# Cached rows of the depthwise convolution first, from their own buffer, and separate input buffers for the convolution of VectorE and of TensorE

## The chip, the cores and the metric

The kernel runs on one core of a Trainium2 chip. The core has a matrix engine (TensorE, PE in the rows), a vector engine (VectorE, DVE), a scalar engine (ScalarE, ACT), GpSimd (POOL) and SyncE (SP), which issues transfers; ScalarE and GpSimd issue transfers as well. Each engine works through its own instructions in order and waits for the others by semaphores. The metric is the time of one execution on the device, in microseconds; less is better.

## The reference

The program is one inference step of a decoder trunk with two layers, for a prompt of 512 tokens and 8 sequences of 4 new tokens each, 544 tokens of 1024 channels in all. The change lies in the first operation of layer 0, a convolution module:

```python
def conformer_conv(h, prev, w_pw1, b_pw1, w_dw, b_dw, ln_g, ln_b, w_pw2, b_pw2):
    u = h @ w_pw1 + b_pw1
    a, g = jnp.split(u, 2, axis=-1)
    u = a * jax.nn.sigmoid(g)
    if prev is None:
        prev = jnp.zeros((u.shape[0], CONV_W - 1, u.shape[2]), u.dtype)
    full = jnp.concatenate([prev.astype(u.dtype), u], axis=1)
    y = lax.conv_general_dilated(full, w_dw[:, None, :].astype(u.dtype), (1,), 'VALID',
                                 dimension_numbers=('NWC', 'WIO', 'NWC'),
                                 feature_group_count=u.shape[-1]) + b_dw
    y = jax.nn.silu(layernorm(y, ln_g, ln_b))
    return y @ w_pw2 + b_pw2, full[:, -(CONV_W - 1):]
```

The filter has CONV_W = 31 taps for each channel. The prompt starts from zeros; each of the 8 sequences starts from 30 cached rows, `state_conv` (8 x 30 x 1024 numbers, 960 KB). The rows that enter the module are normalised and modulated, `h = rmsnorm(x) * (1 + scale) + shift`, where scale, shift and the gate on the result are products of a conditioning vector with `w_ada`. A feed-forward block, projections of keys and values, a compression of cached rows by `w_phi1`, attention and a second feed-forward block follow.

## The kernel before

Channels lie on the 128 partitions, so the 1024 channels are 8 tiles. Matrix products are made in three passes of split numbers: `weights` loads 512 KB into `raw` (4 buffers), ScalarE makes the high part `whi` (L168), VectorE the low part `wlo` (L169), and `products` (L182, L184) multiplies high with high, high with low and low with high. The input is split in the same way: for each of 8 channel tiles VectorE makes `ht` (L542) and `h_lo` (L545), ScalarE `h_hi`. The small `ts` steps of GpSimd (L555, L557, L558) do the modulation for the 32 tokens of the sequences, which the products need for their second part of each row.

`gated_units` makes the convolution's input, one unit for each channel tile f = 0 to 7: 96 matmuls (two products, the gate and the value), the sigmoid on ScalarE, then `up` (L660) and `un` (L663) on VectorE. `up` is the tile for the 512 prompt tokens with 30 zeros ahead, `un` holds the new tokens of the sequences. Between units TensorE does pieces of the modulation, `ada_steps` (L449), whose loads use the `raw` buffers as well.

The convolution of the prompt is divided. For f = 0, 1, 2 VectorE does it, 31 operations for each tile (L736, L738), in `depthwise`. For f = 3 to 7 (`PE_CONV`) TensorE does it in `conv_products`: `up` goes out to DRAM (`up_d`) and comes back as a tile `xt` of shifted rows, GpSimd builds tap matrices `wd4` (L692), and 32 matmuls on quarters of the array (L700; 64 in the trace) make the sum.

The cached rows' share of the sequences' convolution is made in `state_parts`: a load of `state_conv`, 16 transposes on TensorE, four copies (L428), and for each channel tile and each half of the sequences a multiplication on GpSimd into `pr` (L435, two buffers) and a reduction on VectorE into `ys0` (L437), so 16 of each. It runs in the pool "setup". When this pool is closed the pool "compress" takes its place in the buffer: `w1` with the weights of the compression (16 loads of 128 KB, L974), eight small loads `hk` (L993) with the transpose `peT` of them on VectorE (L995), and the gathered cache rows `nat` (L1000) with their transposes (L1013). A tile of "compress" that lies where a tile of "setup" lay waits until that one is no longer read.

The order on each engine is set by a scheduler that plays the program through when the kernel is built; a piece may be put off by a lower priority, and a transfer can be told to be issued behind another one (`issue_after`). Transfers of SyncE and of GpSimd are issued in the order of their queues; one that has to wait holds up those behind it.

Of the kernel before, what the change touches and what calls it, by code (L numbers as in the profile page):

```python
# [7 lines left out]
F32 = mybir.dt.float32  # L8
# [6 lines left out]
P = 128  # L15
D = 1024
KT = D // P
SEQ = 512
# [10 lines left out]
CW = 31  # L29
# [12 lines left out]

TAIL_K = 2
NSTEP = 4
NF = 2
EARLY = 2
SEVEN = (8, 4)
NX = NB + 2
# [5 lines left out]
PE_CONV = (3, 4, 5, 6, 7)  # L54
# [58 lines left out]
class Kernel:  # L113
# [300 lines left out]

    def state_parts(self, sp):

        two = sp.tile([P, 4 * D + 64], F32, name="xt")
        sc = two[:120, :2 * D].rearrange("p (a d) -> p a d", a=2)
        with self.tc.issue_after(self.first_weights):
            self.sy.dma_start(sc, self.A["state_conv"].rearrange("l (a b) w d -> (l b w) a d", a=2))  # L420
        us = two[:, 2 * D:].rearrange("p (f b w) -> p f b w", f=KT, b=NB)
        self.g.memset(us[:, :, :, CW - 1:], 0.0)
        for a in range(2):
            for f0 in range(0, KT, 4):
                pt = self.bank()
                for f in range(4):
                    self.transpose(pt[:, f * 120:(f + 1) * 120], sc[:, a, (f0 + f) * P:(f0 + f + 1) * P])
                self.s.copy(us[:, f0:f0 + 4, a * 4:(a + 1) * 4, :CW - 1],  # L428
                            pt[:, :480].rearrange("p (f b w) -> p f b w", f=4, b=4))
        for f in range(KT):  # L430
            for b0 in range(0, NB, 4):
                uv = us[:, f, b0:b0 + 4]
                win = bass.AP(tensor=uv.tensor, offset=uv.offset, ap=[list(uv.ap[0]), [CW + DS - 2, 4], [1, DS], [1, CW - 1]])
                pr = sp.tile([P, 4, DS, CW - 1], F32, name="pr", bufs=2)
                self.g.tensor_tensor(out=pr, in0=win, in1=self.w_dw[:, :CW - 1, f].unsqueeze(1).unsqueeze(1)  # L435
                                     .broadcast_to([P, 4, DS, CW - 1]), op=ALU.mult)
                self.v.tensor_reduce(out=self.ys0[:, f, b0 * DS:(b0 + 4) * DS], in_=pr.rearrange("p b t w -> p (b t) w"),  # L437
                                     axis=AX.X, op=ALU.add)
# [190 lines left out]
    def gated_units(self, pool, between):  # L629
# [7 lines left out]
        self.ups = []  # L637
        convs = []
        for f in range(KT):
            if f == NF:  # L640
                self.first_weights = self.last_weights
            if f == STATE:
                yield
            cols = [wsrc[:, :, c * D + f * P:c * D + (f + 1) * P] for c in (1, 0)]
# [2 lines left out]
            else:  # L647
# [2 lines left out]
                    next(between, None)  # L650
                pg = self.product(wg, self.h_hi, self.h_lo, KT)
                pa = self.product(wa, self.h_hi, self.h_lo, KT)
            up = pool.tile([P, CW + SEQ], F32, name="up", bufs=4)
            self.ups.append(up)
            g.memset(up[:, :CW - 1], 0.0)
            g.memset(up[:, CW - 1 + SEQ:], 0.0)
# [20 lines left out]
    def conv_products(self, pool, f):  # L677


        n = SEQ + 28  # L680
        up, i = self.ups[f], PE_CONV.index(f)
        vs = self.compress_pool.tile([P, 4, n], F32, name="xt", bufs=3)
        ud = self.up_d[i]
        self.g.dma_start(ud, up)
        for t in range(4):
            src = bass.AP(tensor=ud.tensor, offset=ud.offset + t, ap=[[CW + SEQ, 32], [32 * (CW + SEQ), 4], [1, n]])
            self.g.dma_start(vs[32 * t:32 * t + 32], src)
        wds = []
        for q0 in range(0, 8, 4):

            wd = pool.tile([P, 4, 4, 32], F32, name="wd4", bufs=3)
            self.g.tensor_tensor(out=wd, in0=self.tap.unsqueeze(1).unsqueeze(1).broadcast_to([P, 4, 4, 32]),  # L692
                                 in1=self.w4[:, i, :, q0:q0 + 4].unsqueeze(3).broadcast_to([P, 4, 4, 32]), op=ALU.mult)
            wds.append(wd)

        yield
        pt = self.bank()
        for q in range(8):
            for gg in range(4):
                self.te.matmul(pt[32 * gg:32 * gg + 32, :], wds[q // 4][:, gg, q % 4], vs[:, gg, 4 * q:4 * q + SEQ], start=q == 0, stop=q == 7)  # L700
        self.s.activation(self.y[:, f, :SEQ], pt, AF.Identity, bias=self.b_dw[:, f:f + 1])
        yield
# [42 lines left out]
    def conv_states(self, pool):  # L745
# [2 lines left out]
        g.tensor_copy(uc.rearrange("p f (b t) -> p f b t", t=DS), self.un[:, :, :, DS - 1:])  # L748
        for f0 in range(0, KT, 4):

            both = pool.tile([P, 4, 4, 32], F32, name="wd4", bufs=3).rearrange("p a b n -> p (a b n)")
            cs, cn = both[:32], both[32:32 + NS]
            for f in range(4):
                pt = self.bank("b")
# [861 lines left out]
    def run(self):  # L1616
        tc, A = self.tc, self.A

        def sbuf(name, side="left"):
            return tc.tile_pool(name=name, bufs=1, side=side, reuse_waits="tile")  # L1620

        with sbuf("const") as self.cp, sbuf("norm") as self.np, \
# [17 lines left out]
            with sbuf("conv") as pool:  # L1640
                self.ys0 = pool.tile([P, KT, NS], F32, name="ys0")
                self.conv_pool = pool
                with sbuf("setup", "right") as sp:
                    self.setup(sp)
                    between = self.ada_steps(0, 2)
                    ada1 = itertools.chain(*(self.ada_steps(1, part) for part in (1, 0, 2)))
                    units_ = self.gated_units(pool, between)
                    next(units_)
                    self.state_parts(sp)
                compressing = sbuf("compress", "right")  # L1650
                self.compress_pool = compressing.__enter__()
                next(units_)
# [80 lines left out]
            with sbuf("ffn1") as pool:  # L1733
                u_hi, u_lo = [pool.tile([P, KT, TOK + NX], F32R, name=n, bufs=1) for n in ("a_hi", "a_lo")]
                self.unscaled_shift(3, u_hi, u_lo)
                for f in range(KT):
                    w = self.weights(wsrc[:, :, f * P:(f + 1) * P])
# [44 lines left out]
```

## Time and profile before

| | |
|---|---|
| runs, us | 1664.57, 1669.18, 1670.47; median 1669.18 |
| profiled execution, us | 1666.17, of which the span of the trace is 1664.4 |
| mean granted TensorE clock | 0.972 |
| TensorE busy | 1553.0 us (93%) in 12423 matmuls |
| VectorE busy | 1097.8 us (66%) |
| ScalarE busy | 695.2 us (42%) |
| GpSimd busy | 230.9 us (14%) |

The busy shares are averages over the whole program; the units and the convolution stand in its first 345 us. The chain of waits is followed back from the last instruction: at each step it shows what released the next one.

### The profile page before, as it was taken

What the parts mean: (1) busy time and instruction counts of PE and PEld (TensorE: products, weight loads), DVE (VectorE), ACT (ScalarE), POOL (GpSimd) and SP (SyncE); (2) the same over time, 40 slices, a digit from 0 to 9 for tenths busy, and PEclk for the clock granted to TensorE, in tenths of its full rate; (3) what the DMA queues carried; (4) which work ended last, traced back from release to release, by engine and by line L of the source; (5) the groups of instructions that cost most, each with busy time, mean ns of one, the idle gap of its engine ahead of it and who ended that gap; (6) DMA issues with size and microseconds to landing.
All of it is one profiled execution on the core that took longest, in us unless ns stands there. A gap on an engine that the chain in (4) does not pass through costs nothing.

```text
span 1664.4 us, 31574 instructions
## 1 busy us (share of the span) xinstructions
PE 1553.0 (93%) x12423; PEld 1359.1 (82%) x12423; DVE 1097.8 (66%) x2338; ACT 695.2 (42%) x1443; POOL 230.9 (14%) x267
## 2 busy tenths in 40 slices
PE   6889769999998889999999899999999999999997
PEld 3788337989987888999987777655689999999997
DVE  2799545473338888577657644867856964884866
ACT  4422016232122344245445322746745552552554
POOL 3045420021131021101111000000001210110010
PEclk8899978999999999999999999999999999999999
DMA  8655885374389999933869996747222472333231
GB/s 266 168 145 130 189 242 174 105 237 144 116 199 321 308 300 313 315 103 96 197 206 296 267 272 198 224 149 235 66 64 77 152 227 83 96 109 95 76 93 64
DMA packets 315327, 296.05 MB, mean 178 GB/s; under 512 B 15843, under 2 KB 275053, under 8 KB 310939
## 3 DMA queue, kind: packets, MB, share of 16 engines
q1 hardware_dynamic: 304507, 237.24, 48.7%
q0 software_dynamic: 10368, 56.56, 10.6%
q8 instruction: 98, 1.61, 0.4%
q14 instruction: 50, 0.41, 0.1%
q10 hardware_dynamic: 304, 0.23, 0.1%
HBM read 257.39 MB, written 45.76 MB: 182 GB/s over the span
## 4 chain that ended last, share of the span: by engine, by line
PE 70%; DMA 12%; DVE 11%; issue 3%; ACT 2%; SPq 1%; POOL 0%; ACTq 0%; DVEq 0%
PE g L184 19%; PE g L182 18%; PE g L246 9%; PE t L246 4%; PE t L154 3%; PE t L1019 3%; PE o L1500 2%; DMA raw<-in_w_ada_dram 2%; DVE wlo L195 2%; DMA raw<-in_w_up_dram 2%; PE a L449 2%; DVE y L738 1%; DMA w<-in_w_phi_dram 1%; PE t L1349 1%; PE sc L1479 1%
## 5 line engine op out<-in xcount | busy, mean ns | idle before, releaser
L168 ACT CAST whi<-raw 128x512 fp32r<-128x512 f32 x250 | 149.6, 606 | 399.5 <-PE g L184 269.7
L169 DVE TENSOR_TENSOR wlo<-raw,whi 128x512 fp32r<-128x512 f32 x250 | 175.9, 707 | 142.3 <-ACT whi L168 139.8
L182 PE MATMUL g<-h_hi,whi 128*128 128x256 f32 (+1 forms) x584 | 170.6, 293 | 13.3 <-DVE un L663 8.2
L184 PE MATMUL g<-h_hi,whi 128*128 128x288 f32 (+4 forms) x584 | 174.2, 299 | 0.7 <-ACT h_hi L559 0.7
L184 PE MATMUL g<-h_lo,whi 128*128 128x288 f32 (+4 forms) x584 | 174.0, 298 | 0.4 <-DVE h_lo L560 0.4
L184 PE MATMUL g<-h_hi,wlo 128*128 128x288 f32 (+4 forms) x584 | 173.9, 298 | 0.0
L182 PE MATMUL g<-h_lo,whi 128*128 128x256 f32 (+1 forms) x584 | 168.0, 288 | 0.0
L182 PE MATMUL g<-h_hi,wlo 128*128 128x256 f32 (+1 forms) x584 | 167.8, 287 | 0.0
L182 PEld LDWEIGHTS g<-h_hi,whi 128*128 128x128 f32 x584 | 111.7, 192 | 25.5 <-issue 15.2
L246 PE MATMUL g<-T,whi 128*128 128x272 f32 x656 | 127.7, 291 | 4.5 <-DVE sg L260 3.9
L194 ACT CAST whi<-s 128x512 fp32r<-128x512 f32 x128 | 79.4, 620 | 104.9 <-PE g L246 58.7
L182 PE MATMUL g<-a_hi,whi 128*128 128x256 f32 (+1 forms) x372 | 107.2, 289 | 11.9 <-ACT a_hi L889 5.1
L184 PEld LDWEIGHTS g<-h_hi,whi 128*128 128x128 f32 x584 | 111.8, 192 | 4.0 <-issue 2.9
L184 PEld LDWEIGHTS g<-h_hi,wlo 128*128 128x128 f32 x584 | 111.7, 191 | 3.4 <-issue 3.4
L182 PEld LDWEIGHTS g<-h_lo,whi 128*128 128x128 f32 x584 | 112.1, 192 | 2.8 <-issue 2.7
L184 PEld LDWEIGHTS g<-h_lo,whi 128*128 128x128 f32 x584 | 111.5, 191 | 2.9 <-issue 2.1
L182 PEld LDWEIGHTS g<-h_hi,wlo 128*128 128x128 f32 x584 | 111.9, 192 | 1.3 <-issue 1.0
L184 PE MATMUL g<-a_hi,wlo 128*128 128x288 f32 (+1 forms) x372 | 110.4, 297 | 0.0
L184 PE MATMUL g<-a_hi,whi 128*128 128x288 f32 (+1 forms) x372 | 110.4, 297 | 0.0
L184 PE MATMUL g<-a_lo,whi 128*128 128x288 f32 (+1 forms) x372 | 109.9, 296 | 0.0
L246 PEld LDWEIGHTS g<-T,whi 128*128 128x128 f32 x656 | 103.5, 189 | 6.9 <-DVE sg L260 3.3
L182 PE MATMUL g<-a_hi,wlo 128*128 128x256 f32 (+1 forms) x372 | 105.6, 284 | 2.4 <-DVE wlo L169 2.4
(495 smaller groups left out, 4113.8 us busy)
## 6 DMA issues: line engine op xcount, KB each, us to landing
raw<-in_w_ada_dram SPq DMA_DIRECT2D x96, 512.0 KB
raw<-in_w_gate_dram SPq DMA_DIRECT2D x44, 512.0 KB
raw<-in_w_up_dram SPq DMA_DIRECT2D x44, 512.0 KB
raw<-in_w_down_dram SPq DMA_DIRECT2D x32, 512.0 KB
raw<-in_w_pw_dram SPq DMA_DIRECT2D x24, 512.0 KB
kt_d<-ktr SPq DMA_DIRECT2D x96, 128.0 KB
kt<-kt_d SPq DMA_DIRECT2D x24, 512.0 KB
raw<-in_w_kv_dram SPq DMA_DIRECT2D x20, 512.0 KB
```

What stands on the lines that cost most here:

```text
L154: self.te.transpose(out, in_, self.ident[:n, :n])
L168: self.s.copy(hi[:, :b - a], raw[:, a:b])
L169: self.v.tensor_tensor(out=lo[:, :b - a], in0=raw[:, a:b], in1=hi[:, :b - a].bitcast(F32), op=ALU.subtract)
L182: self.te.matmul(pg[:, 0, :split], a, b[:, i, :split], start=st, stop=sp)
L184: self.te.matmul(pg[:, 1, :tokens - split], a, b[:, i, split:tokens], start=st, stop=sp)
L194: self.s.copy(hi, src)
L195: self.v.tensor_tensor(out=lo, in0=src, in1=hi.bitcast(F32), op=ALU.subtract)
L246: self.te.matmul(out, a[:, i], b(i), start=first and i == 0 and j == 0, stop=i == 3 and j == 2, skip_group_check=not first)
L449: self.te.matmul(pa[32 * j:32 * j + 32, :256], self.cT[:, k, :], w[:, j * 256:(j + 1) * 256], start=k == 0, stop=k == KT - 1)
L738: v.scalar_tensor_tensor(out=ps, in0=x, scalar=w, in1=ps, op0=ALU.mult, op1=ALU.add)
L1019: te.matmul(ph[:, :P], self.w1[:, e, c // 2, c % 2], xv[:, c % 2, c // 2], start=c == 0, stop=c == 15)
L1500: te.matmul(po[rp * HD:(rp + 1) * HD, :256], self.vn[:, br, t, gg * HD:(gg + 1) * HD], pT[:, rp * 256:(rp + 1) * 256], start=br == 0 and t ...
```

## The change

Three things change. `state_parts` is called ahead of the first units instead of behind unit 2; it has a tile of its own, "st", instead of taking one of the buffers named "xt", and its load is issued by GpSimd without a rule that puts it behind the weights of unit 1. The convolution inputs of f = 0, 1, 2 are named "upv" with three buffers, those of f = 3 to 7 "up" with two; before, all shared four. The tap matrices `wd4` have two buffers instead of three.

```diff
     def state_parts(self, sp):
 
-        two = sp.tile([P, 4 * D + 64], F32, name="xt")
+        two = sp.tile([P, 4 * D + 64], F32, name="st")
         sc = two[:120, :2 * D].rearrange("p (a d) -> p a d", a=2)
-        with self.tc.issue_after(self.first_weights):
-            self.sy.dma_start(sc, self.A["state_conv"].rearrange("l (a b) w d -> (l b w) a d", a=2))
+        self.g.dma_start(sc, self.A["state_conv"].rearrange("l (a b) w d -> (l b w) a d", a=2))
...
-            if f == NF:
-                self.first_weights = self.last_weights
...
-            up = pool.tile([P, CW + SEQ], F32, name="up", bufs=4)
+
+            up = pool.tile([P, CW + SEQ], F32, **(dict(name="up", bufs=2) if f in PE_CONV else dict(name="upv", bufs=KT - len(PE_CONV))))
...
-            wd = pool.tile([P, 4, 4, 32], F32, name="wd4", bufs=3)
+            wd = pool.tile([P, 4, 4, 32], F32, name="wd4", bufs=2)
...
-            both = pool.tile([P, 4, 4, 32], F32, name="wd4", bufs=3).rearrange("p a b n -> p (a b n)")
+            both = pool.tile([P, 4, 4, 32], F32, name="wd4", bufs=2).rearrange("p a b n -> p (a b n)")
...
                     units_ = self.gated_units(pool, between)
+                    self.state_parts(sp)
                     next(units_)
-                    self.state_parts(sp)
```

The scheduler makes another order of this. In the changed kernel line numbers are lower by 1 to 3. GpSimd's queue around unit 0, before: the steps `ts` of the modulation stand together behind three tap matrices, the first multiplication `pr` behind unit 0's copy `ut`.

```order
L692 TENSOR_TENSOR wd_1083<-c_small,w_263 128x512
L692 TENSOR_TENSOR wd_1085<-c_small,w_263 128x512
L692 TENSOR_TENSOR wd_1254<-c_small,w_263 128x512
L555 TENSOR_TENSOR ts<-x,mod 128x256
L557 TENSOR_TENSOR ts<-ts,rstd 128x256
L558 TENSOR_TENSOR ts<-ts,mod 128x256
L666 COPY ut<-up 128x30
L435 TENSOR_TENSOR pr<-xt,vec 128x480
```

The same place of GpSimd's queue in the changed kernel.

```order
L689 TENSOR_TENSOR wd_1083<-c_small,w_263 128x512
L689 TENSOR_TENSOR wd_1085<-c_small,w_263 128x512
L433 TENSOR_TENSOR pr<-st,vec 128x480 x2
L553 TENSOR_TENSOR ts<-x,mod 128x256
L555 TENSOR_TENSOR ts<-ts,rstd 128x256
L433 TENSOR_TENSOR pr<-st,vec 128x480 x7
L556 TENSOR_TENSOR ts<-ts,mod 128x256
L433 TENSOR_TENSOR pr<-st,vec 128x480 x7
L997 DMA nat<-in_cache_kv_cmp_dram,rows_78 128x2048 x2
```

All 16 multiplications now stand ahead of unit 0's copy, and nine of them ahead of the last `ts` step.

VectorE's queue at the same place, before, from the last parts of the split input to unit 0's `up`.

```order
L545 SCALAR_TENSOR_TENSOR h_lo_104<-ht_443,mod_105,h_hi_103 128x512
L542 SCALAR_TENSOR_TENSOR ht_451<-x_102,mod_105,rstd_164 128x512
L545 SCALAR_TENSOR_TENSOR h_lo_104<-ht_447,mod_105,h_hi_103 128x512
L545 SCALAR_TENSOR_TENSOR h_lo_104<-ht_451,mod_105,h_hi_103 128x512
L169 TENSOR_TENSOR wlo_565<-raw_562,whi_564 128x512
L169 TENSOR_TENSOR wlo_569<-raw_562,whi_568 128x512
L169 TENSOR_TENSOR wlo_575<-raw_572,whi_574 128x512
L660 SCALAR_TENSOR_TENSOR up_553<-g_456,vec_107,ht_556 128x512
```

The same place of VectorE's queue in the changed kernel.

```order
L540 SCALAR_TENSOR_TENSOR ht_526<-x_102,mod_105,rstd_164 128x512
L435 TENSOR_REDUCE ys0_92<-pr_347 128x16
L543 SCALAR_TENSOR_TENSOR h_lo_104<-ht_522,mod_105,h_hi_103 128x512
L435 TENSOR_REDUCE ys0_92<-pr_350 128x16
L543 SCALAR_TENSOR_TENSOR h_lo_104<-ht_526,mod_105,h_hi_103 128x512
L168 TENSOR_TENSOR wlo_640<-raw_637,whi_639 128x512
L168 TENSOR_TENSOR wlo_644<-raw_637,whi_643 128x512
L435 TENSOR_REDUCE ys0_92<-pr_353 128x16
L986 MEMSET hk_1833 128x64
L168 TENSOR_TENSOR wlo_650<-raw_647,whi_649 128x512
L657 SCALAR_TENSOR_TENSOR upv_628<-g_531,vec_107,ht_631 128x512
```

The last `h_lo` stands behind the fifteenth reduction (`pr_350`), and `wlo_640` and `wlo_644` are unit 1's.

SyncE's queue before, from unit 3's weights (raw 920 and 930) on.

```order
L162 DMA raw_920<-in_w_pw1_dram 128x8x128
L162 DMA raw_930<-in_w_pw1_dram 128x8x128
L447 DMA raw_940<-in_w_ada_dram 128x1024
...
L162 DMA raw_2661<-in_w_pw2_dram 128x8x128
L974 DMA w1_1805<-in_w_phi1_dram 32x8x128 x6
L447 DMA raw_2774<-in_w_ada_dram 128x1024
L974 DMA w1_1805<-in_w_phi1_dram 32x8x128 x10
L447 DMA raw_2780<-in_w_ada_dram 128x1024
L993 DMA hk_1833<-in_pe_cmp_dram 8x64 x8
```

SyncE's queue in the changed kernel, from unit 2's weights (raw 764 and 774) on.

```order
L161 DMA raw_774<-in_w_pw1_dram 128x8x128
L445 DMA raw_785<-in_w_ada_dram 128x1024
L971 DMA w1_1805<-in_w_phi1_dram 32x8x128 x7
L445 DMA raw_791<-in_w_ada_dram 128x1024
L971 DMA w1_1805<-in_w_phi1_dram 32x8x128
L445 DMA raw_797<-in_w_ada_dram 128x1024
L971 DMA w1_1805<-in_w_phi1_dram 32x8x128 x8
L990 DMA hk_1833<-in_pe_cmp_dram 8x64 x3
L445 DMA raw_803<-in_w_ada_dram 128x1024
L990 DMA hk_1833<-in_pe_cmp_dram 8x64 x5
L161 DMA raw_920<-in_w_pw1_dram 128x8x128
```

The compression's weights and the `hk` loads have moved from behind all weights of the units to ahead of unit 3's.

## Rows read from the trace of the kernel before

**Rows 1.** Busy time by stretch: PE, PEld, DVE, ACT, POOL (instructions), PEclk, DMA share, GB/s

```profile
66.80:79.20 12.40, 12.40 (x103) 12.24 (x105) 12.19 (x18) 4.05 (x9) 2.53 (x2) 1.00 0.41 128
95.20:150.00 54.80, 46.62 (x352) 45.24 (x349) 54.80 (x66) 12.03 (x23) 32.48 (x27) 0.94 0.38 107
150.00:180.00 30.00, 30.00 (x254) 20.18 (x255) 28.61 (x48) 5.25 (x9) 22.40 (x31) 1.00 0.99 246
180.00:207.70 27.70, 18.48 (x149) 7.38 (x151) 9.11 (x17) 1.31 (x2) 5.43 (x7) 0.88 0.71 143
207.70:238.70 31.00, 16.33 (x128) 4.84 (x124) 8.73 (x12) 2.42 (x7) 8.06 (x12) 0.67 0.86 259
272.50:331.00 58.50, 58.50 (x466) 56.07 (x470) 32.47 (x65) 25.72 (x43) 3.73 (x5) 0.95 0.42 128
```

**Rows 2.** Timeline of TensorE: start, us, what

```profile
65.35 0.68 PE L154 MATMUL t<-c_small,xt 120*128 120x120 f32 x5
...
66.81 0.37 PE L182 MATMUL g<-h_hi,whi 128*128 128x256 f32 x1
...
79.14 1.50 PE L449 MATMUL a<-raw,cT 128*32 128x256 f32 x24
...
95.16 0.39 PE L182 MATMUL g<-h_hi,whi 128*128 128x256 f32 x1
```

**Rows 3.** TensorE's groups of instructions, 95.2 to 207.7: busy, mean ns, idle before

```profile
L700 PE MATMUL t<-xt,wd 128*32 128x512 f32 x256 | 30.2, 627 | 9.2 <-DMA xt<-up_d 9.2
```

**Rows 4.** What VectorE waited for, 60 to 210: us, times, longest

```profile
DVE peT L995 <- DMA hk<-in_pe_cmp_dram: 18.3, 1, 18.3
```

**Rows 5.** Timeline of SyncE's queue

```profile
150.80 3.44 SPq L974 DMA_DIRECT2D w<-in_w_phi_dram  x6
...
155.95 30.72 SPq L974 DMA_DIRECT2D w<-in_w_phi_dram  x10
...
187.68 11.26 SPq L993 DMA_DIRECT2D hk<-in_pe_cmp_dram  x8
```

**Rows 6.** The chain of waits, 110 to 345: start, us, what

```profile
164.46 22.52 DMA w<-in_w_phi_dram
...
208.95 0.76 DVE up L660
...
229.69 9.09 PE t L700 x64
```

**Rows 7.** Tile pr: durations min/median/max in ns; then idle time ended by its reduce

```profile
L435 POOL TENSOR_TENSOR pr<-xt,vec x16: 1481/1981/2539, 68.0 to 145.2; 128x480 f32<-128x480 f32 x16
L437 DVE TENSOR_REDUCE ys<-pr x16: 637/639/641, 70.2 to 150.9; 128x16 f32<-128x480 f32 x16
...
  DVE ys L437: 15.7, 9
```

**Rows 8.** Timeline of GpSimd

```profile
33.58 3.10 POOL L692 TENSOR_TENSOR wd<-c_small,w 128x512 f32<-128x512 f32 x3 [7.03 <-ACT w L412]
...
46.73 0.96 POOL L558 TENSOR_TENSOR ts<-ts,mod 128x256 f32<-128x256 f32 x1 [8.12 <-DVE mod L460]
...
109.43 1.98 POOL L435 TENSOR_TENSOR pr<-xt,vec 128x480 f32<-128x480 f32 x1 [1.19 <-DVE ys L437]
...
283.00 0.99 POOL L1000 DMA_INDIRECT nat<-in_cache_kv_cmp_dram,rows  x1 [3.95 <-DVE xt L1013]
```

**Rows 9.** Timeline of VectorE

```profile
104.92 0.68 DVE L169 TENSOR_TENSOR wlo<-raw,whi 128x512 fp32r<-128x512 f32 x1
...
109.93 2.02 DVE L169 TENSOR_TENSOR wlo<-raw,whi 128x512 fp32r<-128x512 f32 x1
...
292.87 2.37 DVE L1013 STREAM_TRANSPOSE xt<-nat 128x1024 f32<-128x1024 f32 x2 [0.65 <-PE t L1019]
```

**Rows 10.** Busy time from 40 to 48.7, columns as in rows 1

```profile
40.00:48.70 8.70, 3.30 (x26) 0.69 (x18) 2.58 (x5) 3.31 (x7) 0.96 (x1) 0.50 1.11 295
```

**Rows 11.** The chain of waits, 0 to 110

```profile
35.70 3.62 DMA raw<-in_w_ada_dram
```

More of the change, by code (lines that the diff above doesn't have):

```diff
@@ L44 @@
 NSTEP = 4
-NF = 2
 EARLY = 2
```

## The prediction

> **What bounds the kernel now.** I read the chain of waits first, then busy time by stretch, then what each engine waited for. Unit f below is the pair of products of channel tile f (U0 to U7) with the conversion of its result into the convolution's input.
>
> Between U3's first matmul at 95.16 [rows 2] and 207.7, TensorE was busy 46.62 of 54.80 us, then 30.00 of 30.00, then 18.48 of 27.70 [rows 1]: 17.4 us idle in 112.5. Up to 150 VectorE is the bound: busy 54.80 of 54.80 [rows 1]. After 180 it is VectorE too, but because it stands still: its transpose peT waited once, for 18.3 us, for the hk transfers [rows 4]. These stand in SyncE's queue behind the w_phi loads, which took 30.72 us with one other load among them, and took 11.26 us themselves [rows 5]; the chain shows that wait as 22.52 us of w<-in_w_phi [rows 6]. The w_phi loads could not start before 150.80 [rows 5] because their buffer lies where the cached rows' buffers lay, and GpSimd's last multiply for these starts at 145.2 [rows 7]. Behind this stand VectorE's `up` of U7 at 208.95, a round trip through DRAM for the shifted tile, and the convolution of f=7 at 229.69 [rows 6]; there TensorE was busy only 16.33 of 31.00 us [rows 1].
>
> **What the change removes.** The 16 multiplies `pr` and their 16 reduces leave the stretch 68 to 151. A reduce costs VectorE 639 ns [rows 7], so 10.2 us. A multiply costs more than its own time: while one ran from 109.43 for 1.98 us [rows 8], VectorE's wlo, started at 109.93, took 2.02 us and ended with it; a free one 5 us earlier took 0.68 [rows 9]. So each multiply costs VectorE up to 1.3 us, 16 of them up to 21 us. The Trainium skill, GPSIMD Engine Reference, section Specifications, says that GpSimd's SBUF interfaces are shared with VectorE and contend with VectorE instructions that have two SBUF inputs; the trace agrees (2.02 against 0.68 us). By that rule the cost is not removed but laid on whatever VectorE does beside the multiplies, and in the changed order that is U0's `ht` and `h_lo`; I price this below from rows.
>
> With both gone, and peT fed early, I take U3 to U7 as TensorE's own work. A unit is 79.14 - 66.81 = 12.33 us [rows 2], five are 61.7. The convolutions f=3 to 6 took 30.2 us in 256 matmuls [rows 3], 7.55 each. In the new order U7 is no longer broken up by f=6's convolution, which follows it and fits into the 14.7 idle us while f=7's tile travels [rows 1]. So three convolutions stand in front of U7's end: 22.7. With 1.0 for 12 matmuls of the modulation and a few transposes (24 such matmuls took 1.50 [rows 2]) that is 85.4 against 112.5: **27.1 us earlier**, if U3 starts when it did. The lower bound is the 17.4 idle us alone. VectorE does not take over as bound: 54.80 + 28.61 + 9.11 us busy [rows 1], less 10.2 and 21, leave 61 in 85.
>
> **What it adds.** The multiplies now stand in GpSimd's queue around `ts` of U0: of three tap builds ahead (3.10 us from 33.58 [rows 8]) two are left, so it is free at 35.65; then two multiplies, two `ts` steps (0.96 each, as the third [rows 8]), seven multiplies, the third `ts` step, seven more. At the median 1.98 [rows 7] the third step ends at 35.65 + 3.96 + 1.92 + 13.86 + 0.96 = 56.4; before, at 46.73 + 0.96 = 47.7 [rows 8]. The last seven end at 70.2. VectorE's last `h_lo` stands behind the fifteenth reduce, so I put it there too. After it 18 of U0's 96 matmuls are left (the last two k of the second product, and the last k of the first), 2.3 us: U0 ends at 72.5 instead of 65.35 [rows 2], **+7.2**. Bounds: at the shortest multiply, 1.48 [rows 7], the chain is over at 62 and U0 is late only by its third `ts` step, 51.9 against 47.7: +4.2. At the longest, with VectorE's reduce and one `h_lo` in series each time (2.54 + 0.64 [rows 7], + 0.75 for one like wlo), the last fourteen take 55.0 and U0 ends near 100: +34.5. GpSimd already waited 15.7 us for reduces, 9 times [rows 7], which speaks for series; that a multiply and a VectorE operation end together [rows 8, 9] speaks against it. I take 1.98 because two buffers let the next multiply run beside the reduce.
>
> The state's load, 960 KB, now sits in the loads ahead of U0: at the 295 GB/s of 40 to 48.7 [rows 10] 3.3 us of transfers, where DMA is busy already (share 1.11). I count 0, since GpSimd's lateness covers it; without that cover it is 3.3. The Trainium skill, DMA: Bandwidth & Descriptors, section Issuing engines are not separate DMA queues, says that transfers started by GpSimd and by SyncE run on the same 16 engines and interleave; by it moving the load to GpSimd's queue hides nothing of the 3.3 us, and the share of 1.11 with one queue loading agrees that there is no spare room.
>
> Behind U0 TensorE now meets one step of the modulation whose load waits for the buffer that U1's second wlo frees, two wlo (1.3 us) behind the last `h_lo`: 71.5, plus 3.62 as such a load took [rows 11], 75.1: **+2.6** (0 if it comes early).
>
> U3's weights stand behind w_phi and hk on SyncE. These took 42 us together [rows 5]; but at a DMA share of 0.99 [rows 1], while 66.8 to 79.2 had 0.41 [rows 1]. If they take 42 again, from 70.2, U3's weights land near 118 and U3 loses 13 us; at 295 GB/s the 2 MB take 7 and nothing is lost, since U3 is due at 105. I take 0, nearer the quiet stretch. peT now stands behind U1's `up`; it too can then wait for hk, with the convolution behind it, but 61 us of VectorE work in 85 leave room.
>
> In the output product VectorE's first residual update stood behind a transpose of gathered rows, and does still, now with the gate's bias behind it as well and two further transposes ahead of the second. A gather issued at 283.00 [rows 8] was transposed at 292.87 [rows 9]: 9.9 us. Before, that hid behind matmuls (58.50 of 58.50 busy from 272.5 [rows 1]). Now it costs 0 to 9.9; I take **+4**, a little under half, as it is one wait and partly covered.
>
> **Sum.** -27.1 + 7.2 + 2.6 + 4 = -13.3 us. The profiled execution took 1666.2, 3.0 less than the median of 1669.2; so 1652.9 there and **1656** as a median. Behind 345 the order hardly changes and every stage hangs on the residual stream, so the shift should be carried to the end. A later stage that waits for transfers rather than for the chain could swallow part of it; I count nothing for that, and let the range hold it.
>
> **The rivals.** About 0.5% (8 us) is what a measurement here tells from no change.
> 1. Partial gain, as summed: 1656, its own range 1650 to 1663. Chance 0.42.
> 2. The head hides the multiplies: pace 1.48, U0 +4.2, 1.8 for the modulation, no gather wait: 27.1 - 6 = 21, 1648. For it: VectorE was busy only 2.58 of 8.70 us from 40 to 48.7 [rows 10], so an early start of the multiplies would meet little. Against: every operation of U0's `h_lo` has two SBUF inputs. 0.14.
> 3. Given back: the pace is multiply plus reduce, 2.62. U0's chain ends at 79.2, U0 at 81.5: +16.2 + 2.6, and 8 for the gather: 26.8, nothing left, 1669. For it: the 15.7 us of waits for reduces. U3's late weights give nearly the same. 0.27.
> 4. Slower: the longest pace, 3.93 (above). U0 ends at 99.8: +34.5 + 2.6 - 27.1 = +10, 1679. It decides from an end of U0 past 98. For it: the clock is at 0.50 (its 1.2 GHz level) when U0 starts [rows 10], and matmuls fed one `h_lo` at a time may keep it there. Against: 55 us for fourteen multiplies needs each to be the worst of the sixteen. 0.17.
>
> **The numbers.** Faster: rival 2, and 0.36 of the 0.42 = 0.50; same: 0.27 and the other 0.06 = 0.33; slower 0.17. The range 1643 to 1676 leaves out most of rival 4 and the best of rival 2.
>
> **What the profile will show.** Right: the last `pr` ends near 70, U0's last matmul near 72; no peT wait over a few us; U7's `up` near 192; f=7's convolution ends near 222 instead of 238.7. Wrong: `pr` still running past 78; TensorE idle ahead of U3 with U3's weights as the releaser; a wait of VectorE for a gather in the output product over 8 us; or a lead at 345 that is gone by 700.

## The result: slower by 0.6%

| | before | changed |
|---|---|---|
| median of 12 runs, us | 1665.43 (1655.38 to 1670.47) | 1673.78 (1668.36 to 1682.01) |
| ratio, 95% interval | 1 | 1.0059 (1.0040 to 1.0078) |
| profiled execution, us | 1666.17, span 1664.4 | 1670.97, span 1669.2 |

The change costs 9.8 us (0.0059 of 1665). The time lies inside the range, on the side that had the smallest chance. The line numbers of the changed kernel are 1 to 3 lower: `pr` is L433, its reduce L435, the modulation's matmul L447, `up` L657, `un` L660, TensorE's convolution L697.

First, busy time by stretch. Columns are as in [rows 1]. The stretch in which U0 is fed in the kernel before:

```profile
51.90:65.40 13.50, 13.50 (x91) 13.50 (x92) 8.07 (x12) 5.70 (x8) 0.00 (x0) 0.84 0.61 144
```

The changed kernel, that stretch first:

```profile
51.90:65.40 13.50, 4.28 (x20) 1.99 (x16) 11.21 (x13) 5.01 (x9) 12.11 (x8) 0.50 0.66 181
66.80:79.20 12.40, 11.24 (x68) 11.02 (x68) 12.40 (x14) 3.07 (x5) 7.36 (x4) 0.75 0.00 0
95.20:150.00 54.80, 54.80 (x452) 51.24 (x452) 51.11 (x83) 13.36 (x26) 6.61 (x12) 1.00 0.80 205
150.00:180.00 30.00, 29.56 (x249) 19.54 (x249) 28.32 (x40) 6.03 (x11) 13.46 (x18) 1.00 0.57 141
180.00:207.70 27.70, 27.70 (x235) 19.97 (x237) 13.19 (x29) 5.19 (x9) 11.56 (x16) 1.00 0.41 108
207.70:238.70 31.00, 12.13 (x121) 3.79 (x117) 6.66 (x10) 0.69 (x1) 8.70 (x13) 0.67 0.87 275
```

From 95.2 to 207.7 TensorE now hardly waits: 0.4 us idle of 112.5, where [rows 1] had 17.4 (in the changed kernel this stretch begins in U1, not in U3). That is the gain, and it is there. The loss stands on both sides of it: from 51.9 to 65.4 TensorE is busy 4.28 us instead of 13.50, and behind 207.7 it is 12.13 of 31.00 instead of 16.33.

The waits of VectorE up to 350 confirm one point: peT's 18.3 us [rows 4] are gone.

```profile
DVE peT L992 <- DMA hk<-in_pe_cmp_dram: 0.9, 1, 0.9
```

Next, TensorE's timeline in the changed kernel, at U0's end, at U1's and U3's first matmuls, and behind U7.

```profile
84.10 0.29 PE L183 MATMUL g<-h_hi,wlo 128*128 128x288 f32 x1
...
89.18 1.08 PE L447 MATMUL a<-raw,cT 128*32 128x256 f32 x8 [4.78 <-DMA raw<-in_w_ada_dram]
90.19 0.58 PE L181 MATMUL g<-h_hi,whi 128*128 128x256 f32 x1
...
119.42 0.39 PE L181 MATMUL g<-h_hi,whi 128*128 128x256 f32 x1
...
219.91 1.08 PE L447 MATMUL a<-raw,cT 128*32 128x256 f32 x8 [6.75 <-DMA raw<-in_w_ada_dram]
224.06 1.08 PE L447 MATMUL a<-raw,cT 128*32 128x256 f32 x8 [3.07 <-DMA raw<-in_w_ada_dram]
234.18 1.08 PE L447 MATMUL a<-raw,cT 128*32 128x256 f32 x8 [9.05 <-DMA raw<-in_w_ada_dram]
235.04 7.93 PE L697 MATMUL t<-xt,wd 128*32 128x512 f32 x64
```

Against [rows 2], U0 ends 19.0 us later (84.4 against 65.35), U1 starts 23.4 later, U3 24.3 later. The last four rows show what TensorE does while f=7's tile travels: it waits for three loads of the modulation in turn, the last for 9.05 us, and the convolution of f=7 starts right behind it, not behind its own tile. The tile's four transfers were issued from 213.60 on, the last by 215.84, and the slowest took 11.2 us to land, so the tile lay ready at 227 at the latest. Before, that convolution was released by its tile xt at 229.69 [rows 6], with six steps of the modulation ahead of it; now there are seven. U7's `up`, at 208.95 before, is now at 205.74: from U3's first matmul to it 86.3 us instead of 113.8, 27.5 gained. From U7's `up` to the end of f=7's convolution it is 37.2 instead of 29.8, 7.4 lost. From there to the first matmul of the output product (272.47 before, 282.61 now) it is 39.6 instead of 33.7, 5.9 lost. So the account to that matmul is +24.3 - 27.5 + 7.4 + 5.9 = +10.1 us. Of these 4.8 are left in the profiled span.

The chain of waits of the changed kernel names the same places.

```profile
6.49 18.03 DMA raw<-in_w_ada_dram
24.56 1.08 PE a L447 x8
...
83.29 5.84 DMA raw<-in_w_ada_dram
89.18 1.08 PE a L447 x8
...
204.21 7.00 PE t L697 x64
...
215.24 18.90 DMA raw<-in_w_ada_dram
234.18 1.08 PE a L447 x8
235.26 7.71 PE t L697 x64
```

A load of 512 KB that took 3.62 us ahead of U0 before [rows 11] takes 5.84 at 83.29 and 18.90 at 215.24.

### The profile page after: what moved, and what is told of

Read it like the earlier page. It is cut to its first block, busy times and chain, and to the rows that moved or that the text cites. A ratio compares the mean times of both kernels' runs of the same rounds, so it can differ in the third digit from the quotient of the medians.

```text
span 1669.2 us, 31581 instructions
## 1 busy us (share of the span) xinstructions
PE 1555.4 (93%) x12423; PEld 1359.0 (81%) x12423; DVE 1086.4 (65%) x2338; ACT 696.8 (42%) x1443; POOL 234.2 (14%) x268
## 4 chain that ended last, share of the span: by engine, by line
PE 72%; DMA 11%; DVE 10%; issue 3%; ACT 2%; POOL 1%; SPq 1%; ACTq 0%; DVEq 0%; POOLq 0%
PE g L183 19%; PE g L181 18%; PE g L245 9%; DMA raw<-in_w_ada_dram 4%; PE t L245 3%; PE t L153 3%; PE t L1016 3%; DVE wlo L194 3%; PE o L1497 2%; PE t L697 2%; PE a L447 2%; DMA raw<-in_w_up_dram 2%; DMA raw<-in_w_down_dram 1%; PE t L1346 1%; DVE s L203 1%
## 5 line engine op out<-in xcount | busy, mean ns | idle before, releaser
L168 DVE TENSOR_TENSOR wlo<-raw,whi 128x512 fp32r<-128x512 f32 x250 | 171.9, 692 | 154.7 <-ACT whi L167 144.9
L181 PE MATMUL g<-a_hi,whi 128*128 128x256 f32 (+1 forms) x372 | 107.4, 289 | 10.1 <-ACT a_hi L886 4.4
L181 PE MATMUL g<-a_lo,whi 128*128 128x256 f32 (+1 forms) x372 | 105.4, 284 | 5.5 <-POOL a_lo L887 5.5
```

Of the source, the lines that this page charges most:

```text
L168: self.v.tensor_tensor(out=lo[:, :b - a], in0=raw[:, a:b], in1=hi[:, :b - a].bitcast(F32), op=ALU.subtract)
L181: self.te.matmul(pg[:, 0, :split], a, b[:, i, :split], start=st, stop=sp)
```

## The multiplies around U0

The tile `pr` in the changed kernel: durations min, median, max in ns, then idle time of GpSimd ended by the reduce.

```profile
L433 POOL TENSOR_TENSOR pr<-st,vec x16: 1442/1517/1966, 42.4 to 79.6; 128x480 f32<-128x480 f32 x16
...
  DVE ys L435: 10.0, 7
```

The timeline of GpSimd there:

```profile
40.33 2.09 POOL L689 TENSOR_TENSOR wd<-c_small,w 128x512 f32<-128x512 f32 x2 [29.31 <-ACT w L411]
...
49.04 10.32 POOL L433 TENSOR_TENSOR pr<-st,vec 128x480 f32<-128x480 f32 x7 [1.85 <-DVE ys L435]
59.32 1.09 POOL L556 TENSOR_TENSOR ts<-ts,mod 128x256 f32<-128x256 f32 x1
60.62 1.76 POOL L433 TENSOR_TENSOR pr<-st,vec 128x480 f32<-128x480 f32 x1 [0.20 <-DVE ys L435]
...
67.31 1.57 POOL L433 TENSOR_TENSOR pr<-st,vec 128x480 f32<-128x480 f32 x1 [1.85 <-DVE ys L435]
...
79.58 1.94 POOL L433 TENSOR_TENSOR pr<-st,vec 128x480 f32<-128x480 f32 x1 [1.19 <-DVE ys L435]
```

And of VectorE:

```profile
63.41 3.26 DVE L543 SCALAR_TENSOR_TENSOR h_lo<-ht,mod,h_hi 128x512 fp32r<-128x512 f32 x3
66.59 0.64 DVE L435 TENSOR_REDUCE ys<-pr 128x16 f32<-128x480 f32 x1
...
71.79 3.98 DVE L543 SCALAR_TENSOR_TENSOR h_lo<-ht,mod,h_hi 128x512 fp32r<-128x512 f32 x3
...
80.64 1.42 DVE L543 SCALAR_TENSOR_TENSOR h_lo<-ht,mod,h_hi 128x512 fp32r<-128x512 f32 x1
```

Seven multiplies that start at 49.04 go back to back, 1.47 us each. The last seven, from 60.62 to 81.52, take 20.9 us, 3.0 each, though one takes only 1.6 to 2.0: GpSimd waits up to 1.86 us for a buffer, since the reduce that frees it stands on VectorE behind two or three `ht` or `h_lo`. The last two `h_lo` of the products stand behind two of the last reduces. The whole queue also starts late: GpSimd gets its first tap weights at 40.3, because ScalarE's tap copies (L411) start at 35.98 and not at 29.27.

## The experiments

**Theories.** Theory 1: what is lost, is lost ahead of U1, by the load and the multiplies in the head. Theory 2: the 27.5 us gained are spent behind U7, where the seventh step of the modulation stands ahead of f=7's convolution. Theory 3: the separate input buffers, not the place of the multiplies, made the gain. All ratios are to the kernel before on the same chip, with 95% intervals, from 7 to 12 executions of each changed program; the positions, in us, are those of one profiled execution each.

| | ratio | tap copies start | U0's `un` | U7's `un` | f=7's convolution starts |
|---|---|---|---|---|---|
| before | 1 | 29.3 | 67.1 | 209.6 | 229.7 |
| changed | 1.0059 | 36.0 | 86.0 | 206.4 | 235.0 |
| e1_noload | 1.0023 (0.9991 to 1.0054) | 30.3 | 79.7 | 200.8 | 229.8 |
| e2_nomult | 1.0059 (1.0032 to 1.0087) | 35.5 | 96.8 | 211.1 | 239.4 |
| e3_bufs | 1.0024 (0.9990 to 1.0058) | 28.8 | 65.7 | 207.6 | 227.2 |
| e4_after_u0 | 1.0015 (0.9990 to 1.0041) | 35.3 | 79.3 | 203.5 | 232.3 |
| e5_ada7 | 1.0016 (0.9989 to 1.0043) | 36.6 | 86.7 | 209.2 | 230.5 |
| e6_u0_sp | 0.9968 (0.9944 to 0.9991) | 29.3 | 72.4 | 198.5 | 227.3 |
| e7_u0_sp_ada7 | 0.9925 (0.9889 to 0.9960) | 28.1 | 70.7 | 195.6 | 215.6 |
| e8_u0_sp_ada4 | 0.9979 (0.9949 to 1.0009) | 35.3 | 78.8 | 201.8 | 221.5 |
| e9_u1_sp_ada7 | 0.9966 (0.9943 to 0.9989) | 31.5 | 68.9 | 203.9 | 226.2 |
| e10_u0_nomult | 0.9934 (0.9900 to 0.9969) | 29.4 | 70.6 | 195.6 | 215.3 |
| e11_u0_ada7 | 0.9964 (0.9941 to 0.9987) | 36.2 | 79.8 | 203.3 | 222.6 |

**e1_noload**: the changed kernel without the load of the state.

```diff
-        self.g.dma_start(sc, self.A["state_conv"].rearrange("l (a b) w d -> (l b w) a d", a=2))
+        self.g.memset(sc, 0.0)
```

> The changed kernel, with the load of the cached rows left out (their tile is set to zero instead, so the state's share of the output is of zeros); multiplies, reduces and order stay nearly the same. Theory 1 (the loss is made ahead of unit 1, some 7 us of it by the load in the head and some 17 us by the multiplies): the first tap copy on ScalarE is back near 29 to 30 us from 36, unit 1 starts near 83 instead of 90, and the whole is 4 to 7 us shorter than the changed kernel, so within 4 us of the kernel before. Theory 2 (the head's delay doesn't matter, since the modulation's loads ahead of the convolution of f=7 set the pace, 234 us): unit 1 earlier, but the convolution of f=7 still starts near 235 and the whole stays 8 to 10 us above the kernel before.

Median 1670.64, 0.0036 less than the changed kernel. The tap copies start 5.7 us earlier and U0's `un` stands 6.3 earlier: the load has a price in the head, where the prediction counted 0. The two intervals overlap, so the 0.0036 alone would not show it; e4, e6, e7 and e11 ask again. Theory 2 expected f=7's convolution near 235; it starts at 229.8.

**e2_nomult**: the changed kernel without the 16 multiplies and reduces.

```diff
-        for f in range(KT):
...
-                self.g.tensor_tensor(out=pr, in0=win, in1=self.w_dw[:, :CW - 1, f].unsqueeze(1).unsqueeze(1)
...
+        self.g.memset(self.ys0, 0.0)
```

> The changed kernel without the 16 multiplies and reduces (ys0 is set to zero, so the cached rows' share is left out of the output); the load, transposes and copies stay. Theory 1: unit 1 starts near 73 instead of 90, since only the load's 7 us are left of the head's delay, and the whole is 12 to 17 us shorter than the changed kernel, 3 to 8 us below the kernel before. Theory 2: the convolution of f=7 still starts near 230 or later and the whole is less than 5 us shorter than the changed kernel.

Median 1676.88: no gain, and U0 later still, which neither theory expected. The edit did more than take work away. Timeline of SyncE's queue:

```profile
43.95 1.33 SPq L962 DMA_DIRECT2D w<-in_w_phi_dram  x3
...
58.23 1.09 SPq L962 DMA_DIRECT2D w<-in_w_phi_dram  x2
59.66 0.40 SPq L161 DMA_DIRECT2D raw<-in_w_pw_dram  x1
61.72 7.31 SPq L962 DMA_DIRECT2D w<-in_w_phi_dram  x6
69.13 6.56 SPq L981 DMA_DIRECT2D hk<-in_pe_cmp_dram  x8
75.79 7.43 SPq L161 DMA_DIRECT2D raw<-in_w_pw_dram  x5
```

With the cached rows' buffers free at once, the scheduler put all 16 w_phi loads and the hk loads ahead of most of the units' weights (L161). It says nothing on the price of the multiplies; e10 asks again with these loads held in place.

**e3_bufs**: the kernel before with the three sets of buffers alone, the cached rows in their old place.

```diff
-        two = sp.tile([P, 4 * D + 64], F32, name="xt")
+        two = sp.tile([P, 4 * D + 64], F32, name="st")
...
-            up = pool.tile([P, CW + SEQ], F32, name="up", bufs=4)
+            up = pool.tile([P, CW + SEQ], F32, **(dict(name="up", bufs=2) if f in PE_CONV else dict(name="upv", bufs=KT - len(PE_CONV))))
...
-            wd = pool.tile([P, 4, 4, 32], F32, name="wd4", bufs=3)
+            wd = pool.tile([P, 4, 4, 32], F32, name="wd4", bufs=2)
```

> The kernel before with the buffers of the change alone: the state's own tile, upv and up apart, two wd4; state_parts in its old place with its old load. Theory 1 (the early state frees VectorE and the w_phi loads, and the buffers by themselves do nothing): same as the kernel before within 4 us, the 18 us wait of peT still there. Theory 3 (units 3 to 7 became shorter because VectorE's and TensorE's convolution tiles no longer share buffers): units 3 to 7 near 90 us instead of 113, and 10 us or more below the kernel before.

1671.64, no measurable difference; U7's `un` at 207.6 and the wait of peT as before (17.8 us). Theory 3 falls: the buffers alone make no gain. The place of the cached rows' work makes it: from U2's `un` to U7's it takes 115.3 us in the kernel before and 114.7 here, 86.7 in the changed kernel and 87 to 93 in the runs with that work ahead of U0 or behind it; in e9, where it stands behind U1, it takes 97.5. Whether the early place would gain as much without the buffers was not run.

**e4_after_u0**: the changed kernel with `state_parts` behind unit 0.

```diff
-STATE = 3
+STATE = 1
...
-        self.g.dma_start(sc, self.A["state_conv"].rearrange("l (a b) w d -> (l b w) a d", a=2))
+        with self.tc.issue_after(self.last_weights):
+            self.g.dma_start(sc, self.A["state_conv"].rearrange("l (a b) w d -> (l b w) a d", a=2))
```

with the call of `state_parts` moved behind `next(units_)`.

> The changed kernel with state_parts called behind unit 0 instead of ahead of it, and its load issued behind unit 0's weights. Theory 1: unit 1 starts within 5 us of 66.8 as in the kernel before, units 3 to 7 keep 86 to 92 us, peT hardly waits; the lead at the start of the feed-forward block (350 us) is 10 to 20 us against the kernel before, and the whole 8 to 18 us below it. Theory 2: the convolution of f=7 waits for the modulation's loads as in the changed kernel, starts at 225 or later, and the whole is within 5 us of the kernel before.

1668.59. The load was still issued in the head, at 9.71: `issue_after` did not hold it on GpSimd's queue. So this run leaves the load where it was and moves the transposes, copies, multiplies and reduces; with them the w_phi loads start later, at 100.49 instead of 83.95. The first nine multiplies still run beside U0, from 57.37 to 80.09, but behind the last `ts` step (53.74), not ahead of it. U0's `un` stands 6.7 us earlier, and 0.0044 (7.3 us) come back. Theory 1's numbers did not come: U0's `un` is still 12.2 us later than before, 6.0 of it by the late head, and the whole is no shorter than before. Theory 2's did.

**e5_ada7**: the changed kernel, with the modulation's seventh and later steps ordered behind f=7's convolution.

```diff
-                next(between, None)
+                if f < 2:
+                    next(between, None)
+                else:
+                    with self.tc.issue_after(self.last_conv):
+                        next(between, None)
```

(`last_conv` is the last matmul of L697.)

> The changed kernel with one edge added: the seventh of the modulation's steps behind unit 7 (four matmuls on raw_2877, for which TensorE waited until 234.18) stands behind the convolution of f=7 instead of ahead of it. Theory 2 (the gain of units 3 to 7 is lost at that load): the convolution of f=7 starts when its tile has landed, 224 to 228 instead of 235, the layer norm's reciprocal comes 5 to 9 us earlier than 271.9, and the whole is 4 to 9 us shorter than the changed kernel, so level with the kernel before. Theory 1 alone (all of the loss is the head's): the step only moves, the layer norm waits for something else, and the whole stays within 2 us of the changed kernel.

1666.60, 0.0043 (7.2 us) less than the changed kernel. f=7's convolution is now released by its own tile, as TensorE's timeline shows:

```profile
228.02 1.08 PE L447 MATMUL a<-raw,cT 128*32 128x256 f32 x8 [3.41 <-DMA raw<-in_w_ada_dram]
230.52 8.85 PE L697 MATMUL t<-xt,wd 128*32 128x512 f32 x64 [1.42 <-DMA xt<-up_d]
```

It starts 21.3 us behind U7's `un`, against 28.6 in the changed kernel. Theories 1 and 2 both hold, each for a part; theory 1 alone expected no gain over 2 us here.

**e6_u0_sp**: e4 with the load in SyncE's queue, behind U0's weights, where `issue_after` does hold it.

```diff
-            self.g.dma_start(sc, self.A["state_conv"].rearrange("l (a b) w d -> (l b w) a d", a=2))
+            self.sy.dma_start(sc, self.A["state_conv"].rearrange("l (a b) w d -> (l b w) a d", a=2))
```

> As e4 (state_parts behind unit 0), but the state's load is issued by SyncE behind unit 0's weights, as in the kernel before behind unit 1's. Theory 1: the first tap copy is back at 29 us, unit 0's un at 67 to 72 us instead of 79 in e4, and unit 7's un near 195 to 198; Theory 2: in spite of this the convolution of f=7 is held by the load of the seventh modulation step (19 us of transfer once more), starting 18 us or more behind unit 7's un plus 7 us, near 223; the whole comes 4 to 10 us below e4.

1660.78, faster than before. Against e4 only the load has moved: the tap copies start 6.0 us earlier, U0's `un` stands 6.9 earlier, 0.0047 (7.8 us) in the whole. U0 is still 5.3 us later than in the kernel before; the state's transposes stand among its matmuls there, and TensorE waited 2.22 us of it, to 52.21, for the load.

**e7_u0_sp_ada7**: e6 and e5's edge together.

```diff
-STATE = 3
+STATE = 1
...
+            self.sy.dma_start(sc, self.A["state_conv"].rearrange("l (a b) w d -> (l b w) a d", a=2))
...
+                    with self.tc.issue_after(self.last_conv):
```

> e6 and the edge of e5 together. If the loss of the change is the head's delay and the seventh step's load, each worth what e5 and e6 show, both lie on the path and add: unit 7's un near 196, the convolution of f=7 near 216, the whole 10 to 20 us below the kernel before. If a later stage (the transfers of 500 to 700 us) sets the time, the lead at 500 us is there and is gone at 700, and the whole is within 5 us of the kernel before.

1653.01, 0.9925: it beats both kernels. The tile again releases f=7's convolution:

```profile
213.35 1.08 PE L448 MATMUL a<-raw,cT 128*32 128x256 f32 x8 [3.50 <-DMA raw<-in_w_ada_dram]
215.60 9.15 PE L698 MATMUL t<-xt,wd 128*32 128x512 f32 x64 [1.17 <-DMA xt<-up_d]
```

It starts 14.1 us earlier than in the kernel before (229.69), and the span is 15.8 us shorter, 1648.6 against 1664.4: no later stage swallows the lead.

**e8_u0_sp_ada4**: e7 with the fourth to seventh steps behind f=7's convolution.

```diff
-                if f < 2:
+                if f < 1:
```

> As e7, with the fourth to seventh modulation steps behind the convolution of f=7. Theory 2: the convolution starts when its tile lands, as in e7 or 1 to 3 us earlier; but the raw buffers of these steps are freed later, so their loads move into the layer norm, and what is won in front is lost again there or in the output product: the whole within 4 us of e7.

1662.23. TensorE stands idle for the tile once, 13.40 us, and f=7's convolution follows U7's `un` by 19.7 us, against 20.0 in e7: steps whose loads come in time cost nothing there. The whole is 0.0054 (9.0 us) above e7, more than the 4 expected. In the profiles the output product starts 8.9 us later than in e7 (274.87 against 265.97). Of this 5.9 are there when f=7's convolution starts, and they come from the head: the tap copies start at 35.3, although the load stands behind U0's weights. The other 3.0 come behind the convolution, where the steps now stand, as expected.

**e9_u1_sp_ada7**: e7 with `state_parts` behind unit 1.

```diff
-STATE = 1
+STATE = 2
```

> As e7, with state_parts one unit later: called behind unit 1, the state's load behind unit 1's weights as in the kernel before. If the multiplies cost what VectorE does beside them, as theory 1 has it, they now slow units 1 to 3 instead of 0 to 2, where VectorE has the convolution as well: unit 0's and unit 1's un as in the kernel before (67 and 81), unit 3's near 125 as in e7, and the whole within 4 us of e7. If their place does not matter to VectorE but only to the products' input (rival), 4 to 10 us below e7.

1659.81. U0 and U1 are earlier than in e7 (U1's `un` 82.5 against 91.2), but then the multiplies hold up the compression: peT waits 11.6 us and U7's `un` is 8.3 us later. Its median lies above e7's, where it was expected level or below; the intervals of the ratios overlap.

**e10_u0_nomult**: e7 without multiplies and reduces, the w_phi and hk loads held behind U2's weights.

```diff
-                self.g.tensor_tensor(out=pr, in0=win, in1=self.w_dw[:, :CW - 1, f].unsqueeze(1).unsqueeze(1)
...
+        self.g.memset(self.ys0, 0.0)
...
-                    self.sy.dma_start(self.w1[32 * a:32 * a + 32, e, :, h], src[e, h, a])
+                    with self.tc.issue_after(self.pin):
+                        self.sy.dma_start(self.w1[32 * a:32 * a + 32, e, :, h], src[e, h, a])
```

> e7 without the 16 multiplies and reduces (the cached rows' share is left out of the output), with the loads of w_phi and hk held behind unit 2's weights so that they can't move into the head as in e2. Theory 1: the multiplies still cost e7 the delay between unit 0's un (70.7) and unit 1's (91.2); without them unit 1's un is near 80 to 82, unit 3's near 110 to 114, and the whole is 5 to 12 us below e7, 17 to 25 us below the kernel before. Rival (those 20 us are the modulation's loads or the clock): unit 1's un stays above 86 and the whole within 3 us of e7.

1656.81: not faster than e7, where theory 1 expected 5 to 12 us. U0's `un` is the same (70.6 and 70.7), although eight of e7's multiplies start before it. U1's `un` is 7.9 us earlier (83.3), but U7's stands at 195.6 in both; the profiled execution here was the slowest of its seven, 11 us above the median. Behind unit 0 the multiplies cost nothing that can be measured. Why the 7.9 us are gone by U7 was not tried apart; the held loads can have a part in it.

**e11_u0_ada7**: e4 and e5's edge together, the load in the head.

```diff
+            self.g.dma_start(sc, self.A["state_conv"].rearrange("l (a b) w d -> (l b w) a d", a=2))
...
+                    with self.tc.issue_after(self.last_conv):
```

> e4 (load on GpSimd in the head) with the edge of e5; against e7 only the queue and place of the state's load differ. If the load in the head is what makes it late (theory 1): the first tap copy at 35 to 37 us as in the changed kernel, e4 and e5, and the whole 6 to 9 us above e7, 3 to 6 us below the kernel before. If the late head is a matter of chance and not of the load (e8 had it at 35.3 with the load behind unit 0's weights): the first tap copy can be at 29 us, and the whole is within 4 us of e7.

1658.58, 0.9964. Against e7, which differs by the load alone, 0.0039 (6.5 us) more, and the tap copies are late again (36.2), as theory 1 has it.

**What they add up to.** The cached rows' work ahead of U0: 7.3 us (changed to e4). The load in the head: 7.8 (e4 to e6) and 6.5 (e11 to e7); e1 without it gave 6.0. The seventh step's load: 7.2 (changed to e5), 7.2 (e6 to e7), 8.5 (e4 to e11). Three costs of some 7 us each; from the changed kernel over e4 and e6 to e7 it is 0.0134, 22 us. Each difference has an uncertainty of 0.003 to 0.004, worked out from the two intervals, and is 0.004 to 0.005 itself. The load and the seventh step are carried by their repetition, with the others in and out; the work ahead of U0 stands on one difference, clear of its uncertainty (0.0044 against 0.0032), and on the rows around U0. With all three avoided, e7 is 12 us faster than the kernel before.

## The head

What the load does ahead of 36 us is told by busy time from 8 to 20 us, here of the kernel before:

```profile
8.00:20.00 12.00, 9.02 (x44) 4.84 (x48) 0.80 (x5) 8.48 (x16) 1.35 (x11) 1.00 0.93 285
```

and of the changed kernel:

```profile
8.00:20.00 12.00, 6.67 (x32) 3.19 (x32) 0.77 (x4) 7.46 (x13) 2.40 (x14) 1.00 1.04 284
```

The DMA share goes from 0.93 to 1.04 and the bytes moved do not rise (285 and 284 GB/s), so the state's load takes its part from the others. TensorE, which waits for loads of the modulation there, goes from 9.02 to 6.67 us busy. All five kernels with the load in the head have a share of 1.03 or 1.04, the others 0.84 to 0.93. A second difference goes with it, the pace of TensorE's matmuls. TensorE's timeline in the kernel before:

```profile
14.98 1.12 PE L154 MATMUL t<-c_small,xt 128*128 128x128 f32 x4
...
24.14 0.66 PE L154 MATMUL t<-c_small,xt 128*128 128x128 f32 x4 [0.28 <-DVE x L133]
```

and in the changed one:

```profile
16.45 1.12 PE L153 MATMUL t<-c_small,xt 128*128 128x128 f32 x4
...
30.49 1.11 PE L153 MATMUL t<-c_small,xt 128*128 128x128 f32 x4 [0.28 <-DVE x L132]
```

Before, four transposes fall from 1.12 to 0.66 us from 21.72 on; its timeline shows no wait from 13.73 to there. In the changed kernel TensorE waited for loads five times between 9.8 and 24.56, 0.45 to 1.92 us each, and the same transposes still take 1.11 at 30.49. The granted clock of both kernels from 20 to 30 is given as 1.00 (2.4 GHz). In e4, whose L382 matmuls there take the same 1.44 us as the changed kernel's, busy time by stretch gives 0.50 (1.2 GHz):

```profile
30.00:36.00 6.00, 5.72 (x34) 3.34 (x38) 1.37 (x7) 1.24 (x4) 0.00 (x0) 0.50 0.12 19
```

So, by e4's row and the equal durations, the slow pace is that of the lower level, and the records of the others do not show it. The tap copies start at 35.3 to 36.6 in all five profiles with the load in the head, where the slow pace lasts up to them, and at 28.1 to 31.5 in seven of eight without, where it ends before. The eighth is e8, which is late and slow without the load. Its rows of TensorE:

```profile
23.56 1.12 PE L153 MATMUL t<-c_small,xt 128*128 128x128 f32 x4
...
34.13 0.68 PE L153 MATMUL t<-c_small,vc 124*128 124x124 f32 x2
```

and the same two places in e9, which has the same instructions between them:

```profile
24.00 0.79 PE L153 MATMUL t<-c_small,xt 128*128 128x128 f32 x4
...
30.57 0.43 PE L153 MATMUL t<-c_small,vc 124*128 124x124 f32 x2
```

From the first row to the second it is 10.57 us in e8 and 6.57 in e9, with no wait for a load in either: the slow pace by itself is worth 4.0 us here. In e8 TensorE waits for no load from 15.81 on and the pace stays slow all the same, so the waits are not shown to be its cause. In the changed kernel, then, some 4 of the 6.7 us can be the pace and the rest the waits; this is an estimate from e8 and e9. That the load costs 6 to 8 us in the whole is shown by the pairs above; how it divides, and why the pace stays slow with the load, stays open.

## Why the prediction was wrong, by its steps

At the same marks, measured against predicted: U3 starts 24.3 us later, not 9.8; from there to U7's `up` 27.5 are gained, not 27.1; from `up` to the end of f=7's convolution 7.4 are lost, not 0; from there to the output product 5.9, not 0.

**"27.1 us earlier, if U3 starts when it did": right.** 27.5 from U3's first matmul to U7's `up`. peT's wait fell from 18.3 to 0.9, U3's weights released nothing late, and VectorE did not become the bound (51.11 of 54.80). e3 shows that the buffers alone do not make it. One reading beside it was wrong: f=6's convolution did not break U7 up in the kernel before. U7's matmuls end there at 192.4; f=5's convolution (183.47) stands among them and f=6's (199.01) behind them, ahead of `up`, while now it starts at 204.21 and stands close to `up`. The number holds all the same, since the stretch was measured to `up`.

**"The state's load ... I count 0, since GpSimd's lateness covers it": failed.** It cost 6.5 to 7.8 us, twice the bound of 3.3. The cover was looked for on the engine that uses the data; the transfer took its share from the modulation's loads, which TensorE's in-order work ahead of the tap copies was waiting for, and the tap copies came 6.7 us later. The Trainium skill, DMA: Bandwidth & Descriptors, section Issuing engines are not separate DMA queues, says that transfers of all issuing engines interleave on the same 16 DMA engines. The trace agrees: the DMA share from 8 to 20 us rises from 0.93 to 1.04 with the load on GpSimd's queue, and the loads on SyncE's queue come later.

**"U0 ends at 72.5 instead of 65.35, +7.2": mis-sized, it ends at 84.4.** GpSimd comes free at 42.4, not 35.65: 6.8 us, the late head. Then the chain to the last multiply takes 39.1 us instead of 34.6. "I take 1.98 because two buffers let the next multiply run beside the reduce" is the step that failed in it: the first nine were faster than that, the last seven took 3.0 each, since two buffers do not help where the reduce itself waits behind VectorE operations that the multiplies stretch. In the rows above three `h_lo` take 3.26 and 3.98 us together, where one took 0.75 in the kernel before with no multiply beside it. That is the price which the sentences on contention named and which the pace did not carry. U0 ended between rival 3 (81.5) and rival 4 (98). In e4, with the multiplies behind the last `ts` step, U0's `un` is 6.7 us earlier and the whole 7.3 shorter.

**"+2.6" for the modulation's step behind U0: mis-sized.** Its load took 5.84 us, not 3.62, and TensorE waited 4.78 us.

**"Follows it and fits into the 14.7 idle us while f=7's tile travels": incomplete.** f=6's convolution does fit. But no term stood for the modulation's steps in that gap. TensorE works in order, and the new order has a seventh step there whose load of 18.90 us lands after the tile: 7.2 to 8.5 us, shown three times. This term was put at nothing without a reason.

**"+4" for the gather: wrong place.** VectorE waits for gathered rows 2.3 us in two waits. The 5.9 us lost from f=7's convolution to the product are not waits for modulation loads: TensorE waits 2.1 us for these there, against 2.9 before. 92 of the compression's matmuls on gathered rows (L1016) stand in this stretch instead of 64, the last 28 of them right ahead of the product, 4.89 us; no run took this apart.

**Given back later.** Of the +10.1 at the product 4.8 are left in the profiled span; the medians say 9.8, so this one execution is no measure of the rest.

## What to carry to other kernels

When a step is moved to the front, its load is priced against the transfers that are under way there and what waits for them, not against the engine that uses the data. When a wait is taken away, list what an in-order engine has queued between the place that becomes early and the next thing on the path: a ready tile behind a late load is late. An experiment that removes work also frees its buffers, which can pull other loads forward (e2).

## What the runs showed of the hardware

A load of 512 KB took 3.62 us in one place and 18.90 in another, where the tile loads of the convolution ran beside it. The DMA share was 0.69 from 35.7 to 39.4 around the first, and 0.97 from 215 to 235 around the second. GpSimd's multiply took 1.52 us in the median here and 1.98 before [rows 7]. An `h_lo` of VectorE that started at 79.42, ahead of the multiply at 79.58, took 0.74 us, and that multiply 1.94 instead of 1.47; the `h_lo` that started at 80.64, while it ran, took 1.42. And TensorE's matmuls in the head ran 1.7 times as long as later (1.11 against 0.66 us for four transposes), in the changed kernel still at 30.49, with the granted clock in the rows at 1.00.
